# One layer of a Fourier and gated-delta-rule mixer on one core: each head's preparation and scan made two generators, its block inverse built in place

## The chip, the core and the metric

The kernel runs on one core of a Trainium2 chip. The time is device microseconds of one execution. Engines are called as in the profile: PE (TensorE) multiplies matrices, DVE (VectorE), ACT (ScalarE) and POOL (GpSimd) do elementwise work, SP only issues transfers (DMAs). Each engine runs its own instructions in the order in which the program was built, and waits at an instruction until what it needs is there.

## The reference, cut to what matters

640 tokens (128 of context, 512 latent) are normalized, modulated, and projected by one 2048 x 7216 matrix. The columns give four Fourier groups, and keys, values, queries, gates and decays of 12 heads of 128. A head runs the chunked gated delta rule, forward and backward; the inverse of a triangular matrix is the part that this change rebuilds.

```python
lmat = jnp.where(strict, jnp.einsum("bhncd,bhnsd->bhncs", kb, k) * decay, 0.0)
a = lmat + eye
t_inv = lax.linalg.triangular_solve(a, jnp.broadcast_to(eye, a.shape),
                                    left_side=True, lower=True)
...
def step(s, inp):
    v_new = u_i - jnp.einsum("bhcd,bhde->bhce", w_i, s)
    o_i = (jnp.einsum("bhcd,bhde->bhce", qg_i, s)
           + jnp.einsum("bhcs,bhse->bhce", a_i, v_new))
    s = s * jnp.exp(gl_i)[..., None, None] + jnp.einsum("bhcd,bhce->bhde", kd_i, v_new)
```

Then each branch is gated, an output projection follows, the gated residual and a last norm. Products run as three products of a high and a low part of each operand.

## The kernel before

A startup of about 240 us (modulation, transposes, first projections) is followed by a stream of projection tiles (`stream`, L988: a matmul of 128x128 weights by 320 tokens, three per pair of k), and then by the output projection (L1252) with the gates of its columns on DVE (`out_gates`, L1108). The 12 heads and the four Fourier groups run beside the stream.

A head has three parts. `solve(h)` transposes the keys, multiplies keys by keys (tile `KK`), and inverts the 40 diagonal blocks of 32x32: it writes them to DRAM (`pd`), reads them one block to a partition (`NP`), and runs a serial chain of a product and a reduction on DVE, 14 small ones (L658, L660) and 20 larger ones (L670, L672, with the scratch tiles `tmp` and `YB`), into `XB`. `XB` goes through DRAM (`xd`, L689, L691) into the tile `DD`, which a DVE transpose (L695) completes. `delta(h)` makes the values (`v`), the decay factors (`E`), multiplies them into the key products and the query products (tile `AL`, L726 and L727), joins the 32-blocks to blocks of 64 and 128 by four groups of small matmuls (L742, L755, L770, L777), and then runs the scan: the context step and four latent steps, each with S by K (L807, whose result DVE turns into `r`, L810), S by Q (L814), the inverse by r (L825, ACT gives `vn`), and the state's update (L833, DVE's `S` at L841) and output (L846, DVE's `o` at L853 and L856). `head_out(h)` (L879) gates the result.

The order is made by the loop at the end: a virtual clock advances 0.82 per chunk of the stream, and each of the generators `outs`, `deltas`, `solves`, `fouriers` is stepped when its due time has come. A generator yields a latency and a busy time at each place at which another may work. `done` holds markers by which generators wait for each other: `stream` waits with a new tile of keys or queries until the head two earlier has gone through `delta`. The framework's scheduler then places the instructions of each engine. Tiles with a tag share a buffer, and a new tile in a buffer waits for the last use of the old one.

Of the kernel before, what the change touches and what calls it, by code (L numbers as in the profile page):

```python
# [21 lines left out]
NH = 12  # L22
# [49 lines left out]
def hybrid_step(ctx: ExitStack, tc: tile.TileContext, x_prompt, x_sample, state_ctx, c, c_ctx,  # L72
# [163 lines left out]
        # The scale of the modulation comes first: the gate columns and the keys, values and queries of the first head  # L236
        # are multiplied without the shift, which the tokens share; its product with their columns is added later.
# [204 lines left out]
    # a first result comes back from DRAM, and the product with the shift is added  # L442
# [19 lines left out]
    def gates():  # L462
# [8 lines left out]
        ax, aa, au, lg = [g.tile(W24, F32, tag="ab", name="ab", bufs=4) for _ in range(4)]  # L471
# [110 lines left out]
    # gates wait in DRAM, in the place of the branch outputs that they will multiply  # L582
# [13 lines left out]
    def solve(h):  # L596
# [67 lines left out]
        YB = g.tile([40, 16, 16], F32, tag="YB", name="YB", bufs=1)  # L664
# [24 lines left out]
        SP.dma_start(out=xd, in_=X2)  # L689
        for b in range(4):  # L690
            SP.dma_start(out=DD[32 * b:32 * b + 32, 0:2, :, 32 * b:32 * b + 32].rearrange("p d t c -> p (d t) c"),  # L691
                         in_=xd[10 * b:10 * b + 10].rearrange("u r c -> r u c"))
# [6 lines left out]
    LAT = (1, 2, 3, 4)  # L699

    def delta(h):
        s = st_h[h]
        KT, QT, k = s["KT"], s["QT"], s["k"]
        s["v"] = v = g.tile([P, 5, P], F32, tag="v", name="v", bufs=1)
# [11 lines left out]
        AL = g.tile([P, 2, 5, 2, P], F32, tag="AL", name="AL", bufs=1)  # L716
        for ts in ((0, 1, 2), (3, 4)):
            pk = bank()
            for i, t in enumerate(ts):
                o = toff(t)  # L720
                PE.matmul(pk[:, P * i:P * (i + 1)], lhsT=KT[:, o:o + P], rhs=QT[:, o:o + P], start=True, stop=True)
            for i, t in enumerate(ts):
                E = g.tile([P, 2, P], F32, tag="E", name="E", bufs=2)
                for d in range(2):
                    ACT.activation(E[:, 1 - d], gb[:, d, P * t:P * (t + 1)], AF.Exp, bias=ngg4[:, d, h, t:t + 1])
                DVE.tensor_tensor(AL[:, :, t, 0], s["KK"][:, :, t], E, ALU.mult)  # L726
                DVE.tensor_tensor(AL[:, :, t, 1], pk[:, P * i:P * (i + 1)].unsqueeze(1).broadcast_to([P, 2, P]), E,  # L727
                                  ALU.mult)
                yield 1.50, 0.3
        if h == NH - 1:  # L730
            done.add("E_last")
        # inverse: the blocks of 32 inside those of 64, then the blocks of 64
        pairs = [(slice(32 * b, 32 * b + 32), slice(32 * b, 32 * b + 32)) for b in range(4)]
        def half(x, odd):
            return x.rearrange("p (m b c) -> p m b c", m=2, b=2)[:, :, odd]

        px = bank()
        for t in range(5):
            for d in range(2):
                for m in range(2):  # L740
                    (o, co), (_, ci) = pairs[2 * m + 1 - d], pairs[2 * m + d]
                    PE.matmul(px[o, 32 * t:32 * t + 32], lhsT=AL[:, 1 - d, t, 0, co], rhs=DI[d][:, t, ci],  # L742
                              start=True, stop=True, tile_position=(0, o.start))
        for r, cc in pairs:
            POOL.tensor_copy(AL[r, :, :, 0, cc], DD[r, 1:3, :, cc])
        for b in range(4):
            POOL.tensor_copy(TA[pairs[b][0], :, pairs[b % 2][1]], DD[pairs[b][0], 0 if b < 2 else 3, :, pairs[b][1]])
        pv = px[:, 0:160].rearrange("p (t c) -> p t c", t=5)
        ACT.copy(YT[0:64, :, 0:32], pv[0:64])
        ACT.copy(YT[64:128, :, 32:64], pv[64:128])  # L750
        yield 2.50, 1.4
        px = bank()
        for t in range(5):
            for d in range(2):
                PE.matmul(px[64 * d:64 * d + 64, 64 * t:64 * t + 64], lhsT=YT[:, t, :],  # L755
                          rhs=half(DT[d][:, t, :], 1 - d), start=True, stop=True, tile_position=(0, 64 * d))
        pv = px[:, 0:320].rearrange("p (t c) -> p t c", t=5)
        DVE.transpose(TA[32:64, :, 0:32], pv[0:32, :, 0:32])
        DVE.transpose(TA[64:96, :, 32:64], pv[96:128, :, 32:64])
        for d in range(2):  # L760
            for m in range(2):
                i, o, cc = pairs[2 * d + m][0], pairs[2 * m + d][0], pairs[2 * m + 1 - d][1]
                ACT.copy(AL[o, 1 - d, :, 0, cc], pv[i, :, 32 * m:32 * m + 32])
# [35 lines left out]
        for step in range(-1, 4):  # L799
            tt = (0, 0) if step < 0 else (1 + step, 4 - step)  # L800
            r = None
            if step >= 0:
# [12 lines left out]
                yield 3.00, 0.9  # L815
# [8 lines left out]
            for d in range(2):  # L824
                PE.matmul(pv[:, P * d:P * (d + 1)], lhsT=AL[:, 1 - d, tt[d], 0, :],  # L825
                          rhs=r[:, d] if step >= 0 else v[:, 0, :], start=True, stop=True)
# [18 lines left out]
            for d in range(2):  # L845
                PE.matmul(po[:, P * d:P * (d + 1)], lhsT=AL[:, 1 - d, tt[d], 1, :], rhs=vn[:, d], start=True, stop=True)  # L846
# [15 lines left out]
            yield 3.00, 0.9  # L862
# [38 lines left out]
    def fourier(f):  # L901
# [4 lines left out]
        # 8-point transform over the grid rows  # L906
# [17 lines left out]
        # transform over the channels of the group: cosine and negative sine parts  # L924
# [8 lines left out]
        # transform over the context tokens, and over the grid columns  # L933
# [87 lines left out]
    # program order: projection chunks, and between them the steps of the heads and of the Fourier groups  # L1021
# [75 lines left out]
    # gate of a column group: products on the vector engine, the sum over the rows (and over all partitions) by ones  # L1097
# [59 lines left out]
    # gating, residual, and the sum of squares of a column group  # L1157
# [22 lines left out]
    # emits the work on the gates as far as the vector engine is estimated to have come  # L1180
# [104 lines left out]
    main, tail = stream(), out_stream()  # L1285
    live = [[x(), 0.0] for x in (outs, deltas, solves, fouriers)]
# [47 lines left out]
```

## Time and profile before

| | us |
|---|---|
| runs | 1521.86, 1523.84, 1523.90 (median 1523.84) |
| span of the profiled execution | 1520.9 |
| PE busy | 1385.3 (91%) |
| DVE busy | 1030.4 (68%) |
| ACT busy | 655.0 (43%) |
| POOL busy | 683.2 (45%) |

A row of a wait gives the engine and the instruction that waits, what it waits for, the total in us, the number of times and the longest. A row of a timeline gives the start, the length and the instruction. A row of a window gives the stretch, its length, each engine's busy time with the number of instructions, the granted clock of PE (1.00 is full), the share of the DMA engines and GB/s. A row of a group gives the operation, its shapes and count, the busy time, the mean in ns and the idle time ahead of it.

### The profile page before, as it was taken

How to read it: one execution, taken by the hardware profiler on the slowest of the kernel's cores; microseconds unless marked ns; L12 is line 12 of the kernel's file. 1: busy time of each engine (PE TensorE's matmuls, PEld its weight loads, DVE VectorE, ACT ScalarE, POOL GpSimd, SP SyncE). 2: the span in 40 equal slices, each digit the busy share in tenths (PEclk: the TensorE clock that was granted, in tenths of full speed). 3: DMA queues.
4: the chain of work that ended last, by engine and by line, in shares of the span. 5: the costliest groups of instructions: out<-in, count | busy, mean ns of one | idle time of the engine just before them, and what ended most of it. 6: DMA issues, size and time to landing. Idle time of an engine off the chain costs nothing. (4 is left out here: it accounts for less than half of the span.)

```text
span 1520.9 us, 26471 instructions
## 1 busy us (share of the span) xinstructions
PE 1385.3 (91%) x10052; PEld 1270.7 (84%) x10052; DVE 1030.4 (68%) x1698; ACT 655.0 (43%) x1717; POOL 683.2 (45%) x761
## 2 busy tenths in 40 slices
PE   6999999899898999999998989898999999979866
PEld 5676889788897999998998989898999988757655
DVE  4454347895969595867768585959583444599955
ACT  5344357236262626353544536262633433223234
POOL 2223336445354535354453544454435332364495
PEclk9999999899999999999999999999999999989989
DMA  9999434313233323233332323332324454855523
GB/s 303 295 335 310 150 120 125 88 44 108 63 85 86 86 74 92 77 90 86 89 87 70 92 81 99 85 96 69 98 77 125 135 166 141 302 186 158 174 77 139
DMA packets 242070, 196.18 MB, mean 129 GB/s; under 512 B 43117, under 2 KB 204826, under 8 KB 241814
## 3 DMA queue, kind: packets, MB, share of 16 engines
q1 hardware_dynamic: 121334, 122.65, 25.3%
q10 hardware_dynamic: 120608, 71.84, 16.9%
q8 instruction: 79, 1.29, 0.3%
q14 instruction: 49, 0.40, 0.1%
HBM read 170.47 MB, written 23.98 MB: 128 GB/s over the span
## 5 line engine op out<-in xcount | busy, mean ns | idle before, releaser
L136 POOL TENSOR_TENSOR wlo<-raw,whi 128x512 fp32r<-128x512 f32 (+1 forms) x276 | 395.9, 1441 | 576.3 <-ACT whi L135 457.8
L988 PE MATMUL mbank<-h_hi,whi 128*128 128x320 f32 x1600 | 520.2, 325 | 0.0
L988 PE MATMUL mbank<-h_lo,whi 128*128 128x320 f32 x1600 | 505.5, 316 | 0.0
L988 PE MATMUL mbank<-h_hi,wlo 128*128 128x320 f32 x1600 | 504.0, 315 | 0.0
L988 PEld LDWEIGHTS mbank<-h_hi,whi 128*128 128x128 f32 x1600 | 308.5, 193 | 2.7
L988 PEld LDWEIGHTS mbank<-h_lo,whi 128*128 128x128 f32 x1600 | 307.9, 192 | 0.5
L988 PEld LDWEIGHTS mbank<-h_hi,wlo 128*128 128x128 f32 x1600 | 307.1, 192 | 0.2
L135 ACT CAST whi<-raw 128x512 fp32r<-128x512 f32 (+1 forms) x276 | 167.7, 615 | 195.5 <-POOL wlo L136 50.7
L1108 DVE SCALAR_TENSOR_TENSOR ga<-wg,cz,ga 128x512 f32<-128x512 f32 x120 | 113.3, 1014 | 0.0
L670 DVE TENSOR_TENSOR tmp<-XB,YB 40x1024 f32<-40x1024 f32 (+1 forms) x60 | 107.7, 1796 | 1.3
L670 DVE TENSOR_TENSOR tmp<-NP,XB 40x1024 f32<-40x1024 f32 (+1 forms) x60 | 106.5, 1774 | 1.5
L820 POOL TENSOR_SCALAR kd<-k,edl 128x128 f32<-128x128 f32 x96 | 63.1, 669 | 50.5 <-PE bank L833 50.2
L1252 PE MATMUL bank<-wlo,y_hi 128*128 128x512 f32 x160 | 63.6, 398 | 13.0 <-POOL wlo L136 13.0
L1252 PE MATMUL mbank<-whi,y_hi 128*128 128x512 f32 x160 | 64.9, 406 | 9.7 <-ACT res L1274 7.1
L807 PE MATMUL bank<-S,KT 128*128 128x128 f32 x192 | 36.1, 301 | 39.9 <-DVE S L841 39.8
L548 ACT COPY pj<-mbank 128x128 f32<-128x128 f32 (+2 forms) x99 | 30.2, 340 | 90.8 <-PE mbank L988 49.7
L1252 PE MATMUL mbank<-wlo,y_hi 128*128 128x512 f32 x160 | 63.9, 399 | 5.4 <-POOL wlo L136 4.5
L807 PEld LDWEIGHTS bank<-S,KT 128*128 128x128 f32 x192 | 28.1, 194 | 46.3 <-DVE S L841 45.5
L1252 PE MATMUL bank<-whi,y_hi 128*128 128x512 f32 x160 | 63.8, 399 | 0.0
L1252 PE MATMUL mbank<-whi,y_lo 128*128 128x512 f32 x160 | 63.4, 396 | 0.0
L1252 PE MATMUL bank<-whi,y_lo 128*128 128x512 f32 x160 | 63.3, 396 | 0.0
L672 DVE TENSOR_REDUCE YB<-tmp 40x64 f32<-40x512 f32 (+2 forms) x60 | 59.8, 996 | 1.8
(327 smaller groups left out, 2578.2 us busy)
## 6 DMA issues: line engine op xcount, KB each, us to landing
raw<-in_w_in ACTq DMA_DIRECT2D x104, 512.0 KB
wm<-in_w_mod SPq DMA_DIRECT2D x64, 512.0 KB
wg<-in_w_mod SPq DMA_DIRECT2D x16, 1024.0 KB
raw<-in_w_out ACTq DMA_DIRECT2D x48, 256.0 KB
gb<-gd SPq DMA_DIRECT2D x12, 640.0 KB
yd<-zs SPq DMA_DIRECT2D x16, 320.0 KB
zl<-yd SPq DMA_DIRECT2D x16, 320.0 KB
yd<-zl SPq DMA_DIRECT2D x16, 320.0 KB
```

The lines of the kernel that those rows point to most:

```text
L135: ACT.copy(whi, raw_part)
L136: sub.tensor_tensor(wlo, raw_part, whi, ALU.subtract)
L548: ACT.copy(pj[:, a:b], ps)
L670: DVE.tensor_tensor(tv, A.unsqueeze(2).broadcast_to(s4), B.rearrange("p j c -> p c j").unsqueeze(1).broadcast_to(s4), ALU.mult)
L672: DVE.tensor_reduce(dst, tv, AX.X, ALU.add)
L807: PE.matmul(pks[:, P * d:P * (d + 1)], lhsT=KT[:, a:a + P], rhs=S[:, d], start=True, stop=True)
L820: POOL.tensor_scalar(kd[:, d], k[:, tt[d], :], edl4[:, d, h, tt[d]:tt[d] + 1], 1.0, ALU.mult, ALU.mult)
L988: PE.matmul(pm[:, 0:320], lhsT=w, rhs=h[k][:, a:b], start=n == 0, stop=n == 3 * NK - 1)
L1108: DVE.scalar_tensor_tensor(ga[m], wm[:, q], cm, ga[m], ALU.mult, ALU.add)
L1252: PE.matmul(acc[t], lhsT=a[kk][:, sl], rhs=w, start=kk == order[0] and j == 0, stop=kk == order[-1] and j == 2)
```

## The change

`delta` is split. `prep(h)` holds the values, the products with E and the inverse, `scan(h)` the five steps; each has its own generator, so that `prep` of the next head may stand beside `scan` of this one. For this `v` and the query products (`AT`) have two buffers. The products with E are written in place into the key-product tile `KK`, called `T`, in which the inverse is then built. The DD tile holds the 32x32 blocks without padding (128x4x5x32 in place of 128x4x5x128), which makes L742 a matmul with 32 rows of contraction and L755 twenty matmuls of 32 by 32 in place of ten of 64. The loads of DD now wait in the program for the marker `("dd", h-1)`, set behind the last use of DD by the head before. `YB` uses the buffer of `gr`, the gates' scratch `ab` the buffer of `tmp`. Two latencies of the scan grow (3.40 and 4.00), and the Fourier groups also wait for the second last head. Cut to its core:

```diff
-        ax, aa, au, lg = [g.tile(W24, F32, tag="ab", name="ab", bufs=4) for _ in range(4)]
+        ab = g.tile([P, 4, 24, 5], F32, tag="tmp", name="ab", bufs=1)
+        ax, aa, au, lg = [ab[:, i] for i in range(4)]
...
-    # persistent tiles of the block inverses
-    DD = g.tile([P, 4, 5, P], F32, tag="DD", name="DD")
-    POOL.memset(DD, 0.0)
+
+    DD = g.tile([P, 4, 5, 32], F32, tag="DD", name="DD")
     DI, DT = (DD[:, 0], DD[:, 3]), (DD[:, 2], DD[:, 1])
-    YT = g.tile([P, 5, 64], F32, tag="YT", name="YT")
+    YT = g.tile([P, 5, 32], F32, tag="YT", name="YT")
     TA = g.tile([P, 5, 64], F32, tag="TA", name="TA")
-    for x in (YT, TA):
-        POOL.memset(x, 0.0)
+    POOL.memset(TA, 0.0)
...
-        YB = g.tile([40, 16, 16], F32, tag="YB", name="YB", bufs=1)
+        YB = g.tile([P, 2, 5, 32], F32, tag="gr", name="YB", bufs=1).rearrange("p a b c -> p (a b c)")[0:40, 0:256].rearrange("p (a b) -> p a b", a=16)
...
+        while h and ("dd", h - 1) not in done:
+            yield 2.00, 0
         for b in range(4):
-            SP.dma_start(out=DD[32 * b:32 * b + 32, 0:2, :, 32 * b:32 * b + 32].rearrange("p d t c -> p (d t) c"),
+            SP.dma_start(out=DD[32 * b:32 * b + 32, 0:2].rearrange("p d t c -> p (d t) c"),
                          in_=xd[10 * b:10 * b + 10].rearrange("u r c -> r u c"))
...
-    def delta(h):
+
+    def prep(h):
         s = st_h[h]
-        KT, QT, k = s["KT"], s["QT"], s["k"]
-        s["v"] = v = g.tile([P, 5, P], F32, tag="v", name="v", bufs=1)
+        KT, QT = s["KT"], s["QT"]
+        s["v"] = v = g.tile([P, 5, P], F32, tag="v", name="v", bufs=2)
...
-        AL = g.tile([P, 2, 5, 2, P], F32, tag="AL", name="AL", bufs=1)
+        T = s["KK"]
+        s["AT"] = AT = g.tile([P, 2, 5, P], F32, tag="AT", name="AT", bufs=2)
...
-                DVE.tensor_tensor(AL[:, :, t, 0], s["KK"][:, :, t], E, ALU.mult)
-                DVE.tensor_tensor(AL[:, :, t, 1], pk[:, P * i:P * (i + 1)].unsqueeze(1).broadcast_to([P, 2, P]), E,
+                DVE.tensor_tensor(T[:, :, t], T[:, :, t], E, ALU.mult)
+                DVE.tensor_tensor(AT[:, :, t], pk[:, P * i:P * (i + 1)].unsqueeze(1).broadcast_to([P, 2, P]), E,
...
-                    (o, co), (_, ci) = pairs[2 * m + 1 - d], pairs[2 * m + d]
-                    PE.matmul(px[o, 32 * t:32 * t + 32], lhsT=AL[:, 1 - d, t, 0, co], rhs=DI[d][:, t, ci],
-                              start=True, stop=True, tile_position=(0, o.start))
+                    (o, co), (i, _) = pairs[2 * m + 1 - d], pairs[2 * m + d]
+                    PE.matmul(px[o, 32 * t:32 * t + 32], lhsT=T[i, 1 - d, t, co], rhs=DI[d][i, t, :],
+                              start=True, stop=True, tile_position=(i.start, o.start))
...
+            POOL.tensor_copy(T[r, :, :, cc], DD[r, 1:3])
         for b in range(4):
-            POOL.tensor_copy(TA[pairs[b][0], :, pairs[b % 2][1]], DD[pairs[b][0], 0 if b < 2 else 3, :, pairs[b][1]])
-        pv = px[:, 0:160].rearrange("p (t c) -> p t c", t=5)
-        ACT.copy(YT[0:64, :, 0:32], pv[0:64])
-        ACT.copy(YT[64:128, :, 32:64], pv[64:128])
+            POOL.tensor_copy(TA[pairs[b][0], :, pairs[b % 2][1]], DD[pairs[b][0], 0 if b < 2 else 3])
+        ACT.copy(YT, px[:, 0:160].rearrange("p (t c) -> p t c", t=5))
...
-                PE.matmul(px[64 * d:64 * d + 64, 64 * t:64 * t + 64], lhsT=YT[:, t, :],
-                          rhs=half(DT[d][:, t, :], 1 - d), start=True, stop=True, tile_position=(0, 64 * d))
-        pv = px[:, 0:320].rearrange("p (t c) -> p t c", t=5)
-        DVE.transpose(TA[32:64, :, 0:32], pv[0:32, :, 0:32])
-        DVE.transpose(TA[64:96, :, 32:64], pv[96:128, :, 32:64])
+                for m in range(2):
+                    i, o = pairs[2 * m + 1 - d][0], pairs[2 * d + m][0]
+                    PE.matmul(px[o, 32 * t:32 * t + 32], lhsT=YT[i, t, :], rhs=DT[d][i, t, :],
...
-                ACT.copy(AL[o, 1 - d, :, 0, cc], pv[i, :, 32 * m:32 * m + 32])
+                ACT.copy(T[o, 1 - d, :, cc], pv[i])
+        done.add(("dd", h))
...
+    def scan(h):
+        s = st_h[h]
+        KT, QT, k, v, T, AT = [s[x] for x in ("KT", "QT", "k", "v", "KK", "AT")]
...
-                yield 3.00, 0.9
+                yield 3.40, 0.9
...
-            yield 3.00, 0.9
+            yield 4.00, 0.9
...
-    def deltas():
+    def preps():
         for h in range(NH):
             while not {("v", h), ("q", h), ("solve", h)} <= done:
                 yield 2.00, 0
-            yield from delta(h)
+            yield from prep(h)
+            done.add(("prep", h))
+
+    def scans():
+        for h in range(NH):
+            while ("prep", h) not in done:
+                yield 1.00, 0
+            yield from scan(h)
             done.add(("delta", h))
...
-            while not {("u", f), ("f", f), "E_last"} <= done:
+            while not {("u", f), ("f", f), "E_last", ("delta", NH - 2)} <= done:
...
-    live = [[x(), 0.0] for x in (outs, deltas, solves, fouriers)]
+    live = [[x(), 0.0] for x in (outs, scans, preps, solves, fouriers)]
```

PE, in the scan of a head in the middle of the program. L833 and L846 are the state's update and the output of one step, L807 and L814 S by K and S by Q of the next. Before:

```order
L833 MATMUL bank<-vn,kd 128x128 x2
L846 MATMUL bank<-vn,AL 128x128 x2
L988 MATMUL mbank<-h_hi,whi 128x320
L988 MATMUL mbank<-h_lo,whi 128x320
L988 MATMUL mbank<-h_hi,wlo 128x320
```

and, behind 24 rows of L988 in all,

```order
L988 MATMUL mbank<-h_hi,whi 128x320
L988 MATMUL mbank<-h_lo,whi 128x320
L988 MATMUL mbank<-h_hi,wlo 128x320
L807 MATMUL bank<-S,KT 128x128 x2
L814 MATMUL bank<-S,QT 128x128 x2
L988 MATMUL mbank<-h_hi,whi 128x320
```

24 more rows of L988 stand between L814 and the next L825. Now (L838, L851, L812, L819 and L830 are the old L833, L846, L807, L814 and L825):

```order
L838 MATMUL bank<-vn,kd 128x128 x2
L851 MATMUL bank<-vn,AT 128x128 x2
L993 MATMUL mbank<-h_hi,whi 128x320
L812 MATMUL bank<-S,KT 128x128
L819 MATMUL bank<-S,QT 128x128
L812 MATMUL bank<-S,KT 128x128
L819 MATMUL bank<-S,QT 128x128
L993 MATMUL mbank<-h_lo,whi 128x320
L993 MATMUL mbank<-h_hi,wlo 128x320
L993 MATMUL mbank<-h_hi,whi 128x320
L830 MATMUL bank<-r,KK 128x128 x2
```

One to five projection products stand between the pieces now; the other products of the head stand in one stretch of up to 256 ahead of the head's L742.

DVE, in the chain of `solve` of a head in the middle (L670, L672). L587 is a gate's step, L841, L856 and L810 are the scan's. Before:

```order
L670 TENSOR_TENSOR tmp<-NP,XB 40x1024
L672 TENSOR_REDUCE YB<-tmp 40x8x8
L587 SCALAR_TENSOR_TENSOR zs<-zs,mbank 128x320
L841 SCALAR_TENSOR_TENSOR S<-S,egl,bank 128x128 x2
L856 TENSOR_TENSOR o<-o,bank 128x128 x2
L670 TENSOR_TENSOR tmp<-NP,XB 40x1024
L672 TENSOR_REDUCE YB<-tmp 40x16x8
L810 SCALAR_TENSOR_TENSOR r<-bank,neg_eg,v 128x128 x2
L670 TENSOR_TENSOR tmp<-XB,YB 40x1024
```

Now (L669, L671 are the chain; L729, L730 the products with E; L550, L551, L553 the convolutions of keys and values):

```order
L669 TENSOR_TENSOR tmp<-NP,XB 40x1024
L553 SCALAR_TENSOR_TENSOR KT<-th,KT 128x641
L671 TENSOR_REDUCE YB<-tmp 40x8x8
L730 TENSOR_TENSOR AT<-bank,E 128x2x128
L669 TENSOR_TENSOR tmp<-NP,XB 40x1024
L729 TENSOR_TENSOR KK<-KK,E 128x2x128
L671 TENSOR_REDUCE YB<-tmp 40x8x8
L730 TENSOR_TENSOR AT<-bank,E 128x2x128
L669 TENSOR_TENSOR tmp<-NP,XB 40x1024
L550 SCALAR_TENSOR_TENSOR vT<-pj,cw,vT 128x641
L671 TENSOR_REDUCE YB<-tmp 40x16x8
```

The scan's steps have left this place, and the products with E and the convolutions stand in it. The beginning of the same chain (L657, L659) stands behind the scan of the head before:

```order
L815 SCALAR_TENSOR_TENSOR r<-bank,neg_eg,v 128x128 x2
L846 SCALAR_TENSOR_TENSOR S<-S,egl,bank 128x128 x2
L861 TENSOR_TENSOR o<-o,bank 128x128 x2
L815 SCALAR_TENSOR_TENSOR r<-bank,neg_eg,v 128x128 x2
L858 SCALAR_TENSOR_TENSOR o<-bank,eg,o 128x128 x2
L657 TENSOR_TENSOR tmp<-NP,XB 40x4
L659 TENSOR_REDUCE XB<-tmp 40x4
```

There L815, L846, L861 and L858 are the steps of the scan, and the two pieces belong to neighbouring heads.

More of the change, by code (lines that the diff above doesn't have):

```diff
@@ L733, in delta @@
         pairs = [(slice(32 * b, 32 * b + 32), slice(32 * b, 32 * b + 32)) for b in range(4)]
-        def half(x, odd):
-            return x.rearrange("p (m b c) -> p m b c", m=2, b=2)[:, :, odd]
         px = bank()
@@ L740, in delta @@
                 for m in range(2):
-                    (o, co), (_, ci) = pairs[2 * m + 1 - d], pairs[2 * m + d]
-                    PE.matmul(px[o, 32 * t:32 * t + 32], lhsT=AL[:, 1 - d, t, 0, co], rhs=DI[d][:, t, ci],
-                              start=True, stop=True, tile_position=(0, o.start))
+                    (o, co), (i, _) = pairs[2 * m + 1 - d], pairs[2 * m + d]
+                    PE.matmul(px[o, 32 * t:32 * t + 32], lhsT=T[i, 1 - d, t, co], rhs=DI[d][i, t, :],
+                              start=True, stop=True, tile_position=(i.start, o.start))
         for r, cc in pairs:
-            POOL.tensor_copy(AL[r, :, :, 0, cc], DD[r, 1:3, :, cc])
+            POOL.tensor_copy(T[r, :, :, cc], DD[r, 1:3])
         for b in range(4):
-            POOL.tensor_copy(TA[pairs[b][0], :, pairs[b % 2][1]], DD[pairs[b][0], 0 if b < 2 else 3, :, pairs[b][1]])
-        pv = px[:, 0:160].rearrange("p (t c) -> p t c", t=5)
-        ACT.copy(YT[0:64, :, 0:32], pv[0:64])
-        ACT.copy(YT[64:128, :, 32:64], pv[64:128])
+            POOL.tensor_copy(TA[pairs[b][0], :, pairs[b % 2][1]], DD[pairs[b][0], 0 if b < 2 else 3])
+        ACT.copy(YT, px[:, 0:160].rearrange("p (t c) -> p t c", t=5))
         yield 2.50, 1.4
@@ L754, in delta @@
             for d in range(2):
-                PE.matmul(px[64 * d:64 * d + 64, 64 * t:64 * t + 64], lhsT=YT[:, t, :],
-                          rhs=half(DT[d][:, t, :], 1 - d), start=True, stop=True, tile_position=(0, 64 * d))
-        pv = px[:, 0:320].rearrange("p (t c) -> p t c", t=5)
-        DVE.transpose(TA[32:64, :, 0:32], pv[0:32, :, 0:32])
-        DVE.transpose(TA[64:96, :, 32:64], pv[96:128, :, 32:64])
+                for m in range(2):
+                    i, o = pairs[2 * m + 1 - d][0], pairs[2 * d + m][0]
+                    PE.matmul(px[o, 32 * t:32 * t + 32], lhsT=YT[i, t, :], rhs=DT[d][i, t, :],
+                              start=True, stop=True, tile_position=(i.start, o.start))
+        pv = px[:, 0:160].rearrange("p (t c) -> p t c", t=5)
+        DVE.transpose(TA[32:64, :, 0:32], pv[0:32])
+        DVE.transpose(TA[64:96, :, 32:64], pv[96:128])
         for d in range(2):
@@ L769, in delta @@
             for d, (ra, rb) in enumerate(((lo, up), (up, lo))):
-                PE.matmul(px[rb, 64 * t:64 * t + 64], lhsT=AL[ra, 1 - d, t, 0, rb], rhs=TA[ra, t, :], start=True, stop=True,
+                PE.matmul(px[rb, 64 * t:64 * t + 64], lhsT=T[ra, 1 - d, t, rb], rhs=TA[ra, t, :], start=True, stop=True,
                           tile_position=(ra.start, rb.start))
@@ L776, in delta @@
             for d, (ra, rb) in enumerate(((lo, up), (up, lo))):
-                PE.matmul(px[ra, 64 * t:64 * t + 64], lhsT=ET[rb, t, :], rhs=AL[rb, 1 - d, t, 0, rb], start=True, stop=True,
+                PE.matmul(px[ra, 64 * t:64 * t + 64], lhsT=ET[rb, t, :], rhs=T[rb, 1 - d, t, rb], start=True, stop=True,
                           tile_position=(rb.start, ra.start))
         for d, (ra, rb, cp) in enumerate(((lo, up, DVE.tensor_copy), (up, lo, ACT.copy))):
-            cp(AL[ra, 1 - d, :, 0, rb], px[ra, 0:320].rearrange("p (t c) -> p t c", t=5))
+            cp(T[ra, 1 - d, :, rb], px[ra, 0:320].rearrange("p (t c) -> p t c", t=5))
         yield 2.50, 1.1
@@ L824, in delta @@
             for d in range(2):
-                PE.matmul(pv[:, P * d:P * (d + 1)], lhsT=AL[:, 1 - d, tt[d], 0, :],
+                PE.matmul(pv[:, P * d:P * (d + 1)], lhsT=T[:, 1 - d, tt[d], :],
                           rhs=r[:, d] if step >= 0 else v[:, 0, :], start=True, stop=True)
@@ L845, in delta @@
             for d in range(2):
-                PE.matmul(po[:, P * d:P * (d + 1)], lhsT=AL[:, 1 - d, tt[d], 1, :], rhs=vn[:, d], start=True, stop=True)
+                PE.matmul(po[:, P * d:P * (d + 1)], lhsT=AT[:, 1 - d, tt[d], :], rhs=vn[:, d], start=True, stop=True)
             for d in range(2):
```

## The prediction

> **What bounds the kernel now.** First the page: the totals, then the mean share of TensorE (PE) by stretch.
>
> ```profile
> span 1520.9 us, 26471 instructions
> PE 1385.3 (91%) x10052; PEld 1270.7 (84%) x10052; DVE 1030.4 (68%) x1698; ACT 655.0 (43%) x1717; POOL 683.2 (45%) x761
> ```
>
> ```profile
> core 0: us, PE busy (x) PEld busy (x) DVE busy (x) ACT busy (x) POOL busy (x), PEclk, DMA share, GB/s
> 900.00:1000.00 100.00, 95.28 (x751) 92.62 (x751) 71.10 (x132) 50.83 (x152) 45.04 (x62) 0.98 0.31 84
> 1200.00:1300.00 100.00, 99.33 (x566) 86.14 (x565) 41.74 (x119) 41.45 (x89) 29.30 (x25) 1.00 0.52 166
> 1300.00:1400.00 100.00, 83.76 (x350) 67.38 (x349) 91.48 (x105) 25.14 (x52) 48.27 (x28) 0.91 0.64 218
> ```
>
> Up to about 1300 us PE is the limit; after it VectorE (DVE) is, in the gate products, which the change leaves alone. The change lies in the twelve heads. Each head's inverse begins on PE at L742; first head, two steady ones and the last:
>
> ```profile
> 295.93 0.32 PE L742 MATMUL bank<-DD,AL 128*32 128x32 f32 x2 [7.36 <-DMA DD<-xd]
> ...
> 757.95 0.45 PE L742 MATMUL bank<-DD,AL 128*32 128x32 f32 x30
> ...
> 839.62 0.36 PE L742 MATMUL bank<-DD,AL 128*32 128x32 f32 x20
> ...
> 1191.21 0.39 PE L742 MATMUL bank<-DD,AL 128*32 128x32 f32 x23
> ```
>
> So a steady head takes 81.7 us, and the eleven periods together 1191.21 - 295.93 = 895.3 us. What PE waits for between 240 and 1250 us:
>
> ```profile
> PE bank L807 <- DVE S L841: 39.8, 20, 3.2
> PE bank L742 <- DMA DD<-xd: 7.4, 1, 7.4
> PE bank L825 <- DVE r L810: 4.8, 2, 2.9
> ```
>
> Twenty waits for the state S, 2.0 us each, and one for the inverted blocks DD, in the first head. An idle PE also pays afterwards, in the granted clock:
>
> ```profile
> 296.00:302.00 6.00, 6.00 (x24) 5.54 (x25) 5.72 (x10) 0.00 (x0) 1.94 (x3) 0.51 0.25 72
> 556.00:560.00 4.00, 4.00 (x18) 4.00 (x18) 3.96 (x6) 0.63 (x2) 0.00 (x0) 0.50 0.49 164
> ```
>
> After the 7.36 us wait the clock is half for 6 us, which costs 6 x 0.49 = **2.9 us**; after a wait for S (the second row) it is half for some 4 us too, 1.7 to 2 us lost. [...]
>
> **The chain that the change exposes.** Each head's inverse needs a serial chain on DVE (L658 to L672), then two transfers. In the first head, where little else ran, and in a steady one:
>
> ```profile
> 251.58 0.15 DVE L658 TENSOR_TENSOR tmp<-NP,XB 40x4 f32<-40x4 f32 x1
> ...
> 290.51 1.21 DVE L672 TENSOR_REDUCE XB<-tmp 40x64 f32<-40x1024 f32 x1
> ...
> 291.75 0.28 SPq L689 DMA_DIRECT2D xd<-XB  x1
> ...
> 294.20 1.81 SPq L691 DMA_DIRECT2D DD<-xd  x4
> ...
> 780.66 0.15 DVE L658 TENSOR_TENSOR tmp<-NP,XB 40x4 f32<-40x4 f32 x1
> ...
> 816.66 0.31 SPq L689 DMA_DIRECT2D xd<-XB  x1
> ```
>
> ```profile
> L670 DVE TENSOR_TENSOR tmp<-XB,YB 40x1024 f32<-40x1024 f32 (+1 forms) x60 | 107.7, 1796 | 1.3
> L670 DVE TENSOR_TENSOR tmp<-NP,XB 40x1024 f32<-40x1024 f32 (+1 forms) x60 | 106.5, 1774 | 1.5
> L672 DVE TENSOR_REDUCE YB<-tmp 40x64 f32<-40x512 f32 (+2 forms) x60 | 59.8, 996 | 1.8
> L672 DVE TENSOR_REDUCE XB<-tmp 40x64 f32<-40x512 f32 (+2 forms) x60 | 59.7, 996 | 1.5
> L658 DVE TENSOR_TENSOR tmp<-NP,XB 40x4 f32<-40x4 f32 (+6 forms) x84 | 29.6, 352 | 4.8 <-DMA NP<-pd 3.0
> L660 DVE TENSOR_REDUCE XB<-tmp 40x4 f32<-40x4 f32 (+6 forms) x84 | 19.1, 228 | 2.4
> ```
>
> The six groups add up to 382.4 us, **31.9 us a head**. The first head took 291.75 - 251.58 = 40.2 us with 5.8 of other DVE work in it, counted from the order at the operations' mean durations, so 34 of its own; the steady head took 36.0 us. I take 33. From the issue of xd to L742 it is 295.93 - 291.75 = 4.2 us. In the steady head xd is issued at 816.66 and L742 stands in the order behind 23.0 us of other PE work, at 839.62: the chain has over 18 us of slack, and PE never waits for it.
>
> **The change part by part.** *Removed:* the scan's five steps now stand close together in PE's order (1 to 5 projection products between pieces, 24 before), and run beside nothing of DVE's long chain; the twenty waits for S (39.8 us) and about ten half-clock stretches (17 to 20 us) should mostly go, 57 to 60 us in all. A dense scan exists in the first head of the trace, where its steps cost a few tenths of a microsecond each. *Small edits:* the transpose of DD shrinks from 128x1280 to 128x320:
>
> ```profile
> L695 DVE STREAM_TRANSPOSE DD<-DD 128x1280 f32<-128x1280 f32 x12 | 18.0, 1503 | 4.4 <-DMA DD<-xd 4.3
> ```
>
> At a quarter of the width it saves at most 1.1 us of DVE a head; one ACT copy less, a memset of DD less, smaller matmuls at L742 and L755 (20 of 32 columns in place of 10 of 64). The transpose stands between L742 and L755, where PE has products to do, and I count these at nothing; at most 1.1 us x 12 = 13 us if that cover were gone. YB in gr's buffer holds back the next head's gr load until the chain's last read; gr is used only some 20 us later, so nothing, and the load's few microseconds a head (up to 2 x 11) if not. The wait that the emission of the DD load now has changes its place by one wait of the generator, which SP reaches in time.
>
> *Moved, and this decides:* in the new order **L742 of a head stands right where the scheduler supposes DD to land**, with about 41 products behind the issue of xd in place of 108; and the chain begins only behind DVE work of the scan before, which itself needs PE. So the next L742 cannot come before the last L742 + the PE work up to the release of that scan work + the chain with what is between its operations + the transfer. A product of the projection takes
>
> ```profile
> 608.46 0.31 PE L988 MATMUL mbank<-h_hi,wlo 128*128 128x320 f32 x1
> ...
> 611.98 0.31 PE L988 MATMUL mbank<-h_hi,wlo 128*128 128x320 f32 x1
> ```
>
> 3.52/24 = 0.147 us. A steady period holds
>
> ```profile
> 758.00:839.60 81.60, 77.38 (x618) 75.25 (x617) 58.91 (x100) 38.78 (x111) 39.46 (x50) 0.98 0.31 86
> ```
>
> 77.38 us of busy PE, 384 products (56.4 us) and about 1.7 us lost to half clock: 19.3 us of small matmuls. What stands inside the chain now, counted from the order, at the durations of
>
> ```profile
> L726 DVE TENSOR_TENSOR AL<-KK,E 128x256 f32<-128x256 f32 x60 | 29.1, 497 | 6.7 <-ACT E L725 6.7
> L727 DVE TENSOR_TENSOR AL<-bank,E 128x256 f32<-128x256 f32 x60 | 24.6, 417 | 13.9 <-PE bank L721 13.8
> L552 DVE SCALAR_TENSOR_TENSOR vT<-pj,cw,vT 128x641 f32<-128x641 f32 x12 | 12.5, 1038 | 0.4
> L810 DVE SCALAR_TENSOR_TENSOR r<-bank,neg_eg,v 128x128 f32<-128x128 f32 x96 | 29.2, 340 | 10.8 <-PE bank L807 10.7
> L856 DVE TENSOR_TENSOR o<-o,bank 128x128 f32<-128x128 f32 x96 | 23.4, 275 | 7.2 <-PE bank L846 7.1
> L869 DVE TENSOR_TENSOR o<-o,m 128x640 f32<-128x640 f32 x12 | 10.9, 911 | 11.7 <-POOL m L868 11.7
> ```
>
> In head 5: eight products with E (3 x 0.50 + 5 x 0.42 = 3.6), six convolution steps of K and V at about 1.04 (6.2), ten scan operations of 0.28 to 0.34 (3.1), the scaling of o (0.9): 13.8 us, against some 4 in the steady head above (36.0 - 31.9). The mean of heads 3 to 6 is 13.4.
>
> A period of heads 3 to 6 is then, with 123 products and 14.4 us of small matmuls ahead of the chain's start: 18.1 + 14.4 + 3.0 (half clock after the wait) + 33 + 13.4 + 1.0 (waits inside the chain for ACT and POOL; an estimate, bounds 0 and 3) + 4.7 (transfer 4.2 and a release of 0.5; bounds 4.2 and 6) = **87.6 us**. Against it PE's own work is 381 x 0.147 + 19.3 = 75.3 us: PE waits near 9 us. The other heads by the same sum: head 1 74.5 (59 products, 10 of small work, 14.1 inside), head 2 84.1 (114, 18.8, 6.8), heads 7 and 8 84.8 each (128, 13.9, 10.4), heads 9 and 10 77.9 each (125, 11.9, 5.9). Head 11 is bound by PE: 466 products, 68.5 + 19.3 + 2 = 90. Together 74.5 + 84.1 + 350.4 + 169.6 + 155.8 + 90 = 924.4 us against 895.3: **+29.1**. Behind the last L742 stand 66 products more than before (+9.7), and the first head's chain has 2.5 us less in it (-2.5). The sum is **+36 us** on the profiled execution. Its 1520.9 us span stands 2.9 below the median of the runs, 1523.8, so the forecast is 1560.
>
> **The rivals.** [...] *Slower still:* each step of the dense scan costs PE a microsecond more, because r, vn and S each wait for an engine with a queue (the 4.8 us at L825 in two waits is the row for it); five a head ahead of the chain's start, so the period grows by 4 to 5: 1600. *The change doesn't do what it says:* scan and preparation are made concurrent in name, but the chain stays serial with the scan; that is my forecast's mechanism, so it has no separate price.
>
> **How the numbers follow.** Forecast (1535 to 1590) 0.60, faster 0.18, no change 0.08, slower still 0.14. Within 0.2% is about what a measurement of this kernel can tell from no change (3 us). The range leaves out most of the faster case and the far half of the slower one: 1508 to 1600. Faster 0.18, same 0.08, slower 0.74.
>
> **What would show it.** Right: waits at L742 for DMA DD of 6 to 10 us in heads 2 to 10, a granted clock of 0.5 behind each, periods near 87 in heads 3 to 6 and under 80 in 9 and 10, waits for S nearly gone, DVE busy without a break from the chain's start to xd. Wrong: no wait at L742, so that the period falls to PE's own 75 us; a chain that starts ahead of the scan's end; or a loss behind 1214 us, in the Fourier groups or the gates, of which the sum has only the 9.7 us.

## The result, and the profile after

The changed kernel takes 1585.07 us (median of 4 runs, 1582.95 to 1589.04) against 1523.76 us of the kernel before, run beside it: a ratio of **1.0413, 95% interval [1.0394, 1.0431]**. It is slower by 61 us, where 36 were forecast; 1585 lies inside the range of 1508 to 1600. The totals of its page:

```profile
span 1581.0 us, 26917 instructions
PE 1414.3 (89%) x10292; PEld 1281.1 (81%) x10292; DVE 1015.0 (64%) x1698; ACT 645.6 (41%) x1705; POOL 694.4 (44%) x759
```

PE's busy time grew by 29.0 us and its idle time (span less busy) from 135.6 to 166.7, by 31.1: the 60.1 us of the span. The waits of PE between 240 and 1300 us:

```profile
PE bank L742 <- DMA DD<-xd: 47.3, 10, 9.6
PE mbank L993 <- POOL wlo L136: 22.2, 19, 2.3
PE bank L812 <- DVE S L846: 8.7, 7, 2.3
PE bank L830 <- DVE r L815: 5.7, 8, 1.7
PE bank L742 <- DVE DD L696: 5.3, 2, 2.9
```

The twenty waits for S (39.8 us before) are down to seven, 8.7 us. In their place PE waits at L742 for the blocks DD, ten times, and 19 times for a weight split from POOL (`wlo`, the low part of a tile of weights). On PE's timeline the first head, two of the middle and the last:

```profile
295.77 0.31 PE L742 MATMUL bank<-DD,KK 32*32 32x32 f32 x2 [9.58 <-DMA DD<-xd]
...
715.08 0.31 PE L742 MATMUL bank<-DD,KK 32*32 32x32 f32 x2 [4.84 <-DMA DD<-xd]
...
803.81 0.31 PE L742 MATMUL bank<-DD,KK 32*32 32x32 f32 x2 [5.25 <-DMA DD<-xd]
...
1237.07 0.32 PE L742 MATMUL bank<-DD,KK 32*32 32x32 f32 x15
```

A middle period is 88.7 us, in place of 82. What closes it stands on the timelines of DVE and of SP's queue, inside this period:

```profile
749.17 0.61 DVE L815 SCALAR_TENSOR_TENSOR r<-bank,neg_eg,v 128x128 f32<-128x128 f32 x2 [3.85 <-PE bank L812]
749.70 0.60 DVE L858 SCALAR_TENSOR_TENSOR o<-bank,eg,o 128x128 f32<-128x128 f32 x2
750.21 1.11 DVE L657 TENSOR_TENSOR tmp<-NP,XB 40x4 f32<-40x4 f32 x1
...
798.15 1.21 DVE L671 TENSOR_REDUCE XB<-tmp 40x64 f32<-40x1024 f32 x1
```

```profile
799.50 0.30 SPq L688 DMA_DIRECT2D xd<-XB  x1
799.85 0.31 SPq L600 DMA_DIRECT2D gr<-gb  x1
801.95 1.82 SPq L692 DMA_DIRECT2D DD<-xd  x4
```

DVE sits idle 3.85 us for the scan's product on PE, does the scan's step, and only then begins the chain (L657 at 750.21, 35.1 us behind the last L742). The chain runs nearly without a break to 799.36 (DVE is busy 46.9 of these 49.2 us), and 4.3 us from the issue of xd to L742 close the loop. That is the loop of the forecast, link by link. The scan is dense only in part: in heads 4 to 7 its third and fourth step each stand 31 to 39 products behind the step before, and from head 5 on the last step stands inside the chain.

The windows show the clock behind such a wait and the two stretches on either side of the last L742:

```profile
804.00:812.00 8.00, 8.00 (x110) 7.09 (x108) 1.00 (x2) 1.47 (x4) 4.02 (x9) 0.71 0.25 59
295.80:1237.10 941.30, 853.91 (x6833) 811.66 (x6834) 630.49 (x1098) 398.82 (x1150) 434.70 (x518) 0.96 0.29 80
1237.10:1581.00 343.90, 297.71 (x1499) 247.56 (x1498) 226.52 (x326) 113.63 (x230) 162.13 (x112) 0.93 0.49 163
```

The eleven periods take 941.3 us (895.3 before), the rest 343.9 (329.7 before): +46.0 and +14.2 make the 60.2.

### The profile page after: what moved, and what is told of

Read it like the earlier page. It is cut to its first block, busy times and chain, and to the rows that moved or that the text cites. A ratio compares the mean times of both kernels' runs of the same rounds, so it can differ in the third digit from the quotient of the medians.

```text
span 1581.0 us, 26917 instructions
## 1 busy us (share of the span) xinstructions
PE 1414.3 (89%) x10292; PEld 1281.1 (81%) x10292; DVE 1015.0 (64%) x1698; ACT 645.6 (41%) x1705; POOL 694.4 (44%) x759
## 5 line engine op out<-in xcount | busy, mean ns | idle before, releaser
L136 POOL TENSOR_TENSOR wlo<-raw,whi 128x512 fp32r<-128x512 f32 (+1 forms) x276 | 423.2, 1539 | 488.7 <-ACT whi L135 384.6
L993 PE MATMUL mbank<-h_hi,wlo 128*128 128x320 f32 x1600 | 513.0, 321 | 22.2 <-POOL wlo L136 22.2
L135 ACT CAST whi<-raw 128x512 fp32r<-128x512 f32 (+1 forms) x276 | 166.7, 613 | 227.0 <-PE mbank L993 73.9
L669 DVE TENSOR_TENSOR tmp<-XB,YB 40x1024 f32<-40x1024 f32 (+1 forms) x60 | 111.6, 1861 | 0.8
L669 DVE TENSOR_TENSOR tmp<-NP,XB 40x1024 f32<-40x1024 f32 (+1 forms) x60 | 108.3, 1804 | 0.5
L825 POOL TENSOR_SCALAR kd<-k,edl 128x128 f32<-128x128 f32 x96 | 40.4, 433 | 111.5 <-PE bank L838 111.5
L1264 PE MATMUL mbank<-whi,y_hi 128*128 128x512 f32 x160 | 66.7, 417 | 14.4 <-ACT res L1286 6.6
L1264 PE MATMUL bank<-wlo,y_hi 128*128 128x512 f32 x160 | 64.6, 404 | 11.5 <-POOL wlo L136 11.5
L846 DVE SCALAR_TENSOR_TENSOR S<-S,egl,bank 128x128 f32<-128x128 f32 x72 | 22.5, 341 | 72.2 <-PE bank L838 71.9
L728 ACT ACTIVATE E<-gb,ngg 128x128 f32<-128x128 f32 x120 | 42.6, 397 | 62.7 <-DVE AT L730 31.7
L547 ACT COPY pj<-mbank 128x128 f32<-128x128 f32 (+2 forms) x99 | 29.7, 337 | 88.7 <-POOL wlo L136 50.5
L833 ACT ACTIVATE vn<-bank,s 128x128 f32<-128x128 f32 x120 | 38.3, 367 | 57.7 <-PE bank L830 48.0
```

Source lines behind the costliest of these rows:

```text
L135: ACT.copy(whi, raw_part)
L136: sub.tensor_tensor(wlo, raw_part, whi, ALU.subtract)
L547: ACT.copy(pj[:, a:b], ps)
L669: DVE.tensor_tensor(tv, A.unsqueeze(2).broadcast_to(s4), B.rearrange("p j c -> p c j").unsqueeze(1).broadcast_to(s4), ALU.mult)
L825: POOL.tensor_scalar(kd[:, d], k[:, tt[d], :], edl4[:, d, h, tt[d]:tt[d] + 1], 1.0, ALU.mult, ALU.mult)
L833: ACT.mul(vn[:, d], pv[:, P * d:P * (d + 1)], s["s3"][:, d, tt[d]:tt[d] + 1])
```

## The experiments

Three parts of the change can be undone apart: the split, the buffer that YB shares with gr, and the scan's two longer latencies.

```diff
# one generator (e1, e4, e5, e6)
-            yield from prep(h)
-            done.add(("prep", h))
+            yield from prep(h)
+            yield from scan(h)
+            done.add(("delta", h))
# YB's own tile (e2, e4, e5, e7)
-        YB = g.tile([P, 2, 5, 32], F32, tag="gr", name="YB", bufs=1).rearrange("p a b c -> p (a b c)")[0:40, 0:256].rearrange("p (a b) -> p a b", a=16)
+        YB = g.tile([40, 16, 16], F32, tag="YB", name="YB", bufs=1)
# the old latencies (e3, e4, e6, e7)
-                yield 3.40, 0.9
+                yield 3.00, 0.9
...
-            yield 4.00, 0.9
+            yield 3.00, 0.9
```

Expected of one generator with all else as changed:

> Undoes the split alone: one generator runs prep and then scan of a head, everything else as in the changed kernel (in-place inverse, unpadded blocks, shared buffers, the longer yields). Theory A (the loop from L742 through a dense scan to the start of DVE's chain and back through DD closes only because scan and prep are separate): the scan's steps stand 84, 55 and 10 products apart again, the waits at L742 for DD fall from 47 us to under 10, and the time is 1515 to 1535 us. Rival B (the new inverse itself costs: more small matmuls, POOL's copies waiting for DD with the weight splits behind them): the time stays at 1565 to 1585 us.

of YB's own tile alone:

> Undoes the sharing of a buffer by YB and gr alone: YB has its own tile again, the split stays. Theory A1 (the shared buffer holds back the load of gr, with it the next head's key work, and so makes the scheduler put L742 and the scan where the loop closes): steps of the scan stand 84 products apart from head 4 on, waits at L742 fall under 15 us, 1515 to 1545 us. Theory A2 (the split alone closes the loop): waits at L742 stay near 45 us and the time at 1570 to 1590 us. Rival B: 1570 to 1590 us too, but with the waits gone and POOL's waits in their place.

of the old latencies alone:

> Sets the scan's two latencies back to 3.00 and 3.00 in the changed kernel, nothing else. Theory A: the order has L742 every 288 and 480 products in turn, scans spread by 72 products from head 3 on; waits for DD under 20 us, waits for S back at 20 to 40 us; 1520 to 1550 us. Rival B: 1565 to 1585 us.

and of the new inverse (with the change's smaller edits: the markers, the gates' scratch, two buffers for `v` and `AT`), with all three undone:

> The new inverse alone (in-place key-product tile, unpadded DD, 32x32 products, one ACT copy less), with one generator, YB's own tile and the old yields, so that the order of the heads is that of the kernel before (L742 every 384 products from head 4 on). Theory A: the inverse is off the path, 1518 to 1528 us. Rival B: it costs on PE or POOL, 1545 us or more.

Three combinations were left, run next:

> One generator, YB with its own tile, the longer yields (3.40 and 4.00) kept: between the one-generator run with both (1579 us) and the one with neither (1517 us). Theory Y (the buffer shared by YB and gr holds back the next head's key work, and DVE's chain with it): 1515 to 1530 us, the chain of a steady head begins 20 to 23 us after L742. Theory Z (the longer yields set the scan's steps where S is late): 1570 to 1580 us, waits for S near 56 us.

> One generator, the shared buffer kept, the old yields (3.00 and 3.00). Theory Y: 1565 to 1580 us, the chain begins 27 to 29 us after L742. Theory Z: 1515 to 1530 us, waits for S near 43 us.

> The split with neither of the two: YB with its own tile and the old yields. If the split costs nothing by itself: 1515 to 1530 us. If the split costs by itself (periods of a head that alternate, 290 and 478 products): 1540 to 1560 us, with 80 us or more of waits on PE between 240 and 1280 us, 65 in the kernel before.

All eight, as measured. "Chain" is how far behind the last L742 DVE's chain begins (L657, L658 before) in heads 4 to 10, read from the timelines; "S, r" and "DD" are PE's waits between 240 and 1300 us.

| run | generators | YB | latencies | us | ratio to before, interval | chain | S, r | DD |
|---|---|---|---|---|---|---|---|---|
| before | one | own | 3.0, 3.0 | 1523 to 1524 | 1 | 22 to 23 | 44.6 | 7.4 |
| e4 | one | own | 3.0, 3.0 | 1517.0 | 0.9954 [0.9938, 0.9970] | 20 to 21 | 47.0 | 4.8 |
| e6 | one | shared | 3.0, 3.0 | 1523.9 | 1.0011 [0.9995, 1.0026] | 20 to 21 | 42.8 | 12.0 |
| e1 | one | shared | 3.4, 4.0 | 1579.2 | 1.0346 [1.0319, 1.0374] | 27 to 30 | 63.7 | 11.5 |
| e5 | one | own | 3.4, 4.0 | 1588.3 | 1.0424 [1.0402, 1.0447] | 29 to 33 | 78.9 | 4.4 |
| e7 | two | own | 3.0, 3.0 | 1568.9 | 1.0301 [1.0276, 1.0325] | 17 to 20 and 45 in turn | 43.4 | 4.6 |
| e3 | two | shared | 3.0, 3.0 | 1573.3 | 1.0316 [1.0294, 1.0337] | 16 to 23 and 44 in turn | 35.8 | 17.3 |
| e2 | two | own | 3.4, 4.0 | 1560.3 | 1.0235 [1.0216, 1.0254] | 37 to 42 | 51.3 | 8.9 |
| changed | two | shared | 3.4, 4.0 | 1585.1 | 1.0413 [1.0394, 1.0431] | 35 to 40 | 14.4 | 47.3 |

What follows. **The new inverse costs nothing** (e4, in which the smaller edits stand too: it gains 0.5%, the only run below the kernel before); so rival B is out, though e1 and e3 came into its span of times. **The split alone costs** some 50 us (e7 against e4) and **the latencies alone** 55 (e1 against e6) and 71 (e5 against e4), but both together only 43 with YB's own tile (e2 against e4) and 61 with the shared buffer (changed against e6), so they are no sum. The shared buffer costs 7 us with one generator and the old latencies (e6 against e4) and 25 in the order of the change (changed against e2), and gains 9 in e1 against e5; the 4 us between e3 and e7 lie within their intervals. Theory A of e1 fell by its time: one generator again, L742 every 384 products again, 11.5 us of waits for DD, all in the first two heads, and yet 1579 us, with waits for S in their place. In e2 and e3 theory A had the waits for DD and the spread of the scan right and the time wrong: 1560 us where at most 1545 was expected, 1573 where it was 1550; A2 of e2 (waits near 45 us, 1570 or more) missed as well. Theory Y of e5 and e6 fell; Z held, with e5 8 us above its span. e7 is above both of its spans, so the split costs more than either theory had; its waits on PE up to 1280 us sum to 97 us, against 64 before, and why is not shown. The waits for DD are one of several forms that the loss takes: e2 has two of them left, in the first heads, and is still 36 us slower than the kernel before:

```profile
PE bank L812 <- DVE S L846: 27.7, 16, 3.8
PE bank L830 <- DVE r L815: 23.6, 12, 3.5
PE bank L742 <- DMA DD<-xd: 8.9, 2, 4.5
```

Is the loop real where DD is waited for? Then a longer transfer must lengthen every period:

```diff
         SP.dma_start(out=xd, in_=X2)
+        xe = dram.tile([40, 32, 32], F32, tag="xe", name="xe", bufs=2)
+        SP.dma_start(out=xe, in_=xd)
...
-                         in_=xd[10 * b:10 * b + 10].rearrange("u r c -> r u c"))
+                         in_=xe[10 * b:10 * b + 10].rearrange("u r c -> r u c"))
```

> The changed kernel with one more DRAM copy between XB and DD (xd to xe, then DD from xe). Its order has a dense scan in every head (steps at 67, 74, 82 and 90 products behind L742) and L742 every 384 products. By the loop (L742, dense scan, chain, transfer, L742) the transfer grows by 2 to 3 us and every period of heads 2 to 10 with it: waits at L742 of 60 to 100 us in all, periods of 84 to 90 us, 1575 to 1610 us. If PE's own work sets the period, the same as the changed kernel within 5 us, 1580 to 1590, with longer waits at L742 and shorter ones elsewhere.

Measured: **1628.2 us, ratio 1.0681 [1.0653, 1.0710]**, above the expected span; the waits at L742 lie in their span, the periods are longer than expected. SP's queue and PE in a middle head (L690 is the added copy, L744 the old L742):

```profile
834.33 0.30 SPq L688 DMA_DIRECT2D xd<-XB  x1
...
836.79 0.48 SPq L690 DMA_DIRECT2D xe<-xd  x1
...
839.30 1.84 SPq L694 DMA_DIRECT2D DD<-xe  x4
```

```profile
841.45 0.26 PE L744 MATMUL bank<-DD,KK 32*32 32x32 f32 x1 [7.45 <-DMA DD<-xe]
```

From the issue of xd to L744 it is 7.1 us, 2.8 more than the 4.3 of the changed kernel; PE's waits for DD sum to 84.2 us over twelve heads, and heads 3 to 9 take 92.0 to 93.7 us each (80.7 to 88.7 in the changed kernel). PE has the products to fill that time and can't: the loop sets the period. Beyond the 2.8 us, the chain begins at 39.5 to 40.9 us behind L742 in heads 3 to 10, later than in most heads of the changed kernel; the order had moved with the copy, so the run isn't a change of the transfer alone, and only the 2.8 us are the transfer's.

The last four runs ask what the latencies do, on the kernel of e4, with nothing else changed.

> The kernel of the inverse alone (one generator, own YB, 1517 us) with only the scan's first latency raised from 3.00 to 3.40. Its steps stand 156, 234, 300 and 307 products behind L742 (156, 228, 294, 301 in the kernel of the inverse alone; 162, 246, 301, 310 with both latencies raised, 1588 us). If the cost grows with the distance (the longer the scan is spread, the later the next chain begins): 1530 to 1560 us, the chain beginning 23 to 27 us after L742. If this latency costs nothing: 1515 to 1525 us. If it is the one that costs: over 1570 us.

> The same with only the second latency raised, from 3.00 to 4.00; steps 162, 240, 300 and 307 products behind L742. If the cost grows with the distance: 1545 to 1580 us. If it is the one that costs: over 1580 us; if it costs nothing: 1515 to 1525 us.

> The same with both latencies at 2.00; steps 150, 210, 270 and 301 products behind L742. If the cost grows with the distance alone: at or below 1517 us, down to 1495. If the place of the S updates between the chain's operations decides, which the order has behind the fourth and the eighth larger product here: 1515 to 1550 us with waits for S of 45 to 70 us.

> The same with both latencies at 1.20; steps 144 to 148, 192, 240 and 282 to 288 products behind L742, L742 every 366 and 402 products in turn. If the cost grows with the distance alone: below the run with 2.00. If the place of the S updates decides (three of them between larger products of the chain here): slower than with 2.00, 1530 to 1570 us, with more than 70 us of waits for S and r.

Measured: e9 1560.7 us (1.0245 [1.0228, 1.0262]), e10 1576.2 (1.0346 [1.0331, 1.0362]), e11 1556.2 (1.0213 [1.0197, 1.0228]), e12 1552.5 (1.0180 [1.0151, 1.0209]). Longer and shorter latencies are both 35 to 59 us worse than 3.00, so distance alone isn't the cause: e9 and e10 came near the spans that it gives (with the chain at 29 to 31 us in e9, where 23 to 27 was expected), but e11, expected at or below 1517, is far above. e12 is not slower than e11, and its waits for S and r are 39.5 us and not over 70, so the number of S updates inside the chain isn't either. All four share something else: in e9, e10 and e11 the chain begins 29 to 33 us behind L742, in e12 18 and 28 to 30 in turn, against 20 to 21 in e4. The order of DVE in a middle head says why. e4, and then e5:

```
L781 COPY KK<-bank 64x5x64
L792 TENSOR_SCALAR q_7743<-bank 128x5
L657 TENSOR_TENSOR tmp<-NP,XB 40x4
...
L550 SCALAR_TENSOR_TENSOR QT<-pj,cw,QT 128x641
```

```
L781 COPY KK<-bank 64x5x64
L792 TENSOR_SCALAR q_7736<-bank 128x5
L550 SCALAR_TENSOR_TENSOR QT<-pj,cw,QT 128x641
L551 SCALAR_TENSOR_TENSOR QT<-pj,cw,QT 128x641
L553 SCALAR_TENSOR_TENSOR QT<-th,QT 128x641
L865 TENSOR_TENSOR o<-o,bank 128x128
L657 TENSOR_TENSOR tmp<-NP,XB 40x4
```

In the kernel before, in e4 and in e6 the chain's first product stands, from head 4 on, ahead of the queries' convolution (in the kernel before one of its operations is ahead of the chain); in e1, e5, e9, e10 and e11 behind the whole of it in each of these heads, in e12 in every second one. The convolution waits for ACT in e5, 18.2 us in seven waits between 560 and 1200 us; e4 has no such wait there. The timelines of e4 and of e5 at this place:

```profile
780.12 0.17 DVE L792 TENSOR_SCALAR q<-bank 128x5 f32<-128x5 f32 x1 [6.05 <-PE bank L788]
780.30 0.16 DVE L657 TENSOR_TENSOR tmp<-NP,XB 40x4 f32<-40x4 f32 x1
```

```profile
809.96 0.17 DVE L792 TENSOR_SCALAR q<-bank 128x5 f32<-128x5 f32 x1 [3.12 <-PE bank L788]
812.42 0.89 DVE L550 SCALAR_TENSOR_TENSOR QT<-pj,cw,QT 128x641 f32<-128x641 f32 x1 [2.29 <-ACT QT L549]
813.34 1.85 DVE L551 SCALAR_TENSOR_TENSOR QT<-pj,cw,QT 128x641 f32<-128x641 f32 x1
816.00 0.83 DVE L553 SCALAR_TENSOR_TENSOR QT<-th,QT 128x641 f32<-128x641 f32 x1 [0.81 <-ACT th L552]
816.75 0.28 DVE L865 TENSOR_TENSOR o<-o,bank 128x128 f32<-128x128 f32 x1
816.94 0.15 DVE L657 TENSOR_TENSOR tmp<-NP,XB 40x4 f32<-40x4 f32 x1
```

From L792 to the chain 0.2 us in e4, 7.0 in e5. The S updates of the scan stand inside the chain, so a chain that begins 9 us later brings S later, and PE, which gets to L812 only 6 to 18 products (0.9 to 2.6 us) later, waits: 76.5 us for S in e5,

```profile
PE bank L812 <- DVE S L846: 76.5, 23, 7.1
PE bank L755 <- ACT YT L748: 10.2, 8, 4.3
```

and 42.7 in e4:

```profile
PE bank L812 <- DVE S L846: 42.7, 23, 4.2
```

That the place of L657 is the cause fits the runs with one generator: three with the chain ahead, 1517 to 1524 us, five with it behind, 1556 to 1588, and e12 with both, 1552.5. But no run moved it alone, so it is argued and not shown, and two runs say that it isn't all. In e11 the waits for S and r are only 9.6 us more than in e4 (56.6 against 47.0), with 17.2 us for ACT's YT at L755 beside them, and the time is 39 us longer. In e12 the later heads with the chain ahead take 82.3 to 82.7 us for 366 products, those with it behind 88.0 to 88.2 for 402; at 0.147 us a product both are some 3.5 us above e4's 81.5 to 81.9 for 384, so within that run the place doesn't part the heads. Why a latency of 3.00 puts it ahead, and the others don't, stays open.

## Why the prediction was right, point by point

*The way and the place: right.* The scan's place ahead of the chain was read from the order, and the waits at L742, half clock behind those that end heads 1 to 8 (0.54 to 0.79 over the 6 to 8 us behind each), and the vanishing of most waits for S came. Some of the named signs did not: 6 to 10 us at L742 in heads 2 to 10 were 2.8 to 5.3 in heads 2 to 9 and none in head 10, and heads 9 and 10 took over 83 us and not under 80. The periods, forecast and measured:

| head | 1 | 2 | 3 to 6 | 7, 8 | 9, 10 | 11 | sum |
|---|---|---|---|---|---|---|---|
| forecast, us | 74.5 | 84.1 | 87.6 each | 84.8 each | 77.9 each | 90.0 | 924.4 |
| measured, us | 71.4 | 87.6 | 87.3, 86.4, 86.7, 88.7 | 87.0, 80.7 | 83.9, 83.5 | 98.2 | 941.3 |

*The loop's terms: right in the mean of heads 3 to 6, and in part by luck.* The chain's own work was taken as 33 us; its six groups sum to 398.9 us, 33.2 a head. The transfer with its release was taken as 4.7 us and measured 4.3 to 4.6 in heads 3 to 6, from the chain's end. From L742 to the chain's start the sum has 35.5 us, and 52.1 from there to the next L742. Heads 5 and 6 have 34.8 and 35.1, then 51.9 and 53.6. Heads 3 and 4 have 38.7 and 38.8, then 48.5 and 47.6: two misses of 3 to 5 us that cancel.

*The half clock's price: too large in the mean.* Taken as 3.0 us; the windows behind the waits that end heads 1 to 8 give 1.5 to 3.0, 2.1 in the mean, for instance 7.5 x 0.40 = 3.0 behind the one at 628 us and 7 x 0.24 = 1.7 behind the one at 542:

```profile
628.50:636.00 7.50, 7.50 (x66) 6.81 (x65) 1.00 (x2) 1.71 (x4) 5.33 (x10) 0.60 0.33 83
542.00:549.00 7.00, 7.00 (x106) 6.16 (x106) 0.51 (x1) 1.85 (x4) 5.50 (x10) 0.76 0.36 90
```

Four of the eight windows give 1.5 to 1.7; the other four give 2.3 to 3.0.

*PE's wait at L742: forecast near 9 us, measured 3.5 to 5.3 in heads 3 to 8.* PE's idle time in a whole period is near the 9 (7.3 to 9.1 us in heads 3 to 6), but 2.6 to 4.2 of it went to waits for the weight splits from POOL (22.2 us in all; before, there was no such row).

*Where the 24 us lie that the sum missed: terms of the wrong size, in the last heads above all.* Heads 9 and 10 took 11.6 us more than summed. Of it 10.4 stand from L742 to the chain's start, summed as 33.3 us and measured as 39.7 and 37.3: PE ran 140 and 135 products there in place of 125, and waited 2.9 us for the transposed DD in head 9, 1.3 for YT and 2.1 for KK in head 10. Head 11, summed as PE's work with 2 us of loss, took 8.2 more; PE is idle 6.9 us in it, 2.4 for the transposed DD and 3.5 for S. The order has the scan spread again in heads 9 to 11, and waits for S come back:

```profile
1207.40 0.49 PE L812 MATMUL bank<-S,KT 128*128 128x128 f32 x2 [1.21 <-DVE S L846]
1210.14 0.49 PE L812 MATMUL bank<-S,KT 128*128 128x128 f32 x2 [2.26 <-DVE S L846]
```

I had priced these heads as if the scan were dense; the S waits themselves are only 0.5, 2.5 and 3.5 us of the three. Head 2 gives 3.5 more, heads 1 and 3 to 8 6.3 less, so the periods are 16.9 above the sum. The part behind the last L742 was taken as +9.7 and came out as +14.2 (4.5 more), and the gain of 2.5 in the first head didn't come (L742 at 295.77, before at 295.93): 16.9 + 4.5 + 2.3 = 23.7, which with the 36.3 of the sum makes the 60.

*The zero for YB's buffer: wrong in this order.* I wrote that gr is used some 20 us later. The last of gr's loads goes out at 799.85 us, and DVE's timeline has

```profile
802.19 0.49 DVE L632 TENSOR_TENSOR gr<-gr,gg 128x320 f32<-128x320 f32 x1 [1.05 <-DMA gr<-gb]
```

so its first use stands 2.3 us behind the load and waits for it, 1.05 us here. e2, with the buffer undone, is 25 us faster, but its order is another (the scan's steps stand 84 products apart), so the 25 us are not the price of this wait alone. In the one-generator order with the old latencies the same edit costs 7 (e6 against e4).

*The rival "faster"*: the waits for S went, 31 us of them, the half clock didn't (0.96 in the window of the eleven periods, 0.97 before), and no order that was tried with the split gives less than 1560. No run shows a length of a wait under which the clock stays full: in the changed kernel it was 0.73 over the 6.4 us behind the 3.52 us wait at 971.48 and 1.00 over the 6.6 us behind the 2.79 us one at 1055.37, and in the kernel before 0.67 over the 5.2 us behind a 2.74 us wait for S at 652.73 and 1.00 over the 7.2 us behind a 3.23 us one at 637.79. The zeros for the smaller inverse held in the order of e4.

## What to carry to other kernels

When a generator or a latency is touched, read from the built order where the long serial chain of the second engine now begins, behind which instruction, and what that one waits for; the runs with one generator differ by up to 71 us with nearly the same work. A wait that disappears from one line is no gain until the sum of idle time is smaller: here 39.8 us of waits for S became 47.3 of waits for DD, and with one edit undone 51 of waits for S and r. Keep parts of a change apart: the new inverse with the smaller edits was worth 0.5% and was hidden under a loss of 4%.

## What the runs showed of the hardware that was not expected

The half clock lasted for different times behind different waits: 6 us at 0.51 behind the 7.36 us wait of the kernel before; behind the 5.25 us wait at 803.81 here it was half for 4.6 us and full behind that:

```profile
804.00:808.60 4.60, 4.60 (x19) 4.15 (x18) 1.00 (x2) 0.66 (x2) 0.90 (x3) 0.50 0.10 16
808.70:812.00 3.30, 3.30 (x92) 2.83 (x91) 0.00 (x0) 0.81 (x2) 3.03 (x7) 1.00 0.45 120
```

A small product on DVE took seven times its shortest time: the chain's first, 40x4, takes 0.15 us at 780.66 of the kernel before, and 1.11 us at 750.21 of the changed one; the group of these small products goes from 352 to 487 ns in the mean:

```profile
L657 DVE TENSOR_TENSOR tmp<-NP,XB 40x4 f32<-40x4 f32 (+6 forms) x84 | 40.9, 487 | 1.3
```

The trace shows what stands beside the long ones, a weight split on POOL (L136):

```profile
750.01 1.29 POOL L136 TENSOR_TENSOR wlo<-raw,whi 128x512 fp32r<-128x512 f32 x1 [1.20 <-ACT whi L135]
751.92 1.29 POOL L136 TENSOR_TENSOR wlo<-raw,whi 128x512 fp32r<-128x512 f32 x1 [0.62 <-ACT whi L135]
```

```profile
751.95 1.32 DVE L657 TENSOR_TENSOR tmp<-NP,XB 40x36 f32<-40x36 f32 x1
```

The product at 750.21 begins inside the first split and ends at its end; the one at 751.95 does the same with the second. Of the 84 small products of the changed kernel, 18 take more than twice the shortest of their size, and all 18 begin while such a split runs and end 0.02 to 0.4 us behind it; so do all five of the kernel before. No run moved the splits away, so this is read from the traces and not shown by an experiment.
